# Adding the halves of attention's outputs with accumulating transfers

## The chip, the cores and the metric

The kernel runs on one core of one Trainium2 chip. A core has five engines with an instruction queue each: TensorE (PE; its weight loads are shown apart as PEld), VectorE (DVE), ScalarE (ACT), GpSimd (POOL) and SyncE (SP), and 16 DMA engines behind the queues that issue transfers (here SP, ACT and POOL). The metric is the device time of one execution in microseconds (us), lower is better.

## The reference

One layer of a hybrid decoder, 2048 tokens of width 1024 in float32: attention and pooling side by side, a gated MLP with a causal convolution, and a gated embedding. The change lies in attention. It has 8 heads of 64 channels. Each query attends to three dilated windows, and the three results are weighted by their softmax denominators:

```python
DIL_PATTERNS = ((128, 1), (512, 4), (2048, 16))
...
def _dilated_attention(q, k, v, slopes):
    """Mixture of dilations: branch outputs weighted by their softmax denominators."""
    for window, dil in DIL_PATTERNS:
        o, m, d = _dilated_branch(q, k, v, slopes, window, dil)
    ...
    w = d * jnp.exp(m - jnp.max(m, axis=0, keepdims=True))
    w = w / jnp.sum(w, axis=0, keepdims=True)
    return jnp.sum(w[..., None] * o, axis=0)
...
def reference(...):
    hn = _rmsnorm(h, ln_mix[i])
    z = hn @ w_in[i]                      # q, k, v, u
    att = _dilated_attention(q, k, v, slopes)
    pool = _multiscale_pool(u, pool_w[i], pool_scale[i])
    h = h + jnp.concatenate([att, pool], axis=-1) @ w_out[i]
    ...                                   # MLP, embedding, final norm
```

The kernel folds the second and third window into one "far" part, so that each query has a "near" and a "far" result.

## The kernel before

Three phases run one after the other: projection (to about 400 us of the span), attention (to about 698 us), and the rest. [...]

Attention walks through 128 steps: 8 heads of 16 query blocks of 128 tokens. Two heads make a pair (32 steps), and four steps make a group. `CFG["ord"]` is a table of stages with a lag each; in step `s` the loop issues, in the order of the table, every stage for the block `s - lag`. Since the schedule of this phase is manual, that is the order of each engine's queue. The stages, with the names in the profile:

- `B`, `A`: take buffers (`tt` for scores, `ee` for exponentials).
- `N`, `F`: near scores (tile `sn`, L574 and L575) and far scores (`sf`, L563 and L564) on TensorE. All near scores share one PSUM bank, in two halves.
- `nm`, `fm`: add the bias and take the minimum (the scores are negated), on VectorE (L579, L585).
- `ne`, `fe`: exponentials with their sums, on ScalarE (L591, L595), each followed by a short read of the sum.
- `T`: the exponentials are turned by TensorE in blocks of 128x128 into `tp` (L605).
- `h`, `l`: high part on ScalarE (`pth`, L618) and low part on VectorE (`ptl`, L622).
- `V`, `W`: the products with the values into `o`, 128 x 512 per group (L633 near, L647 far). A group takes four steps: parts 0 and 1 are far, parts 2 and 3 near.
- `o`, `p`: take the result out of PSUM. The values carry high and low parts side by side, so that 64 of the 128 rows of `o` have the product with one and 64 that with the other, and the two halves must be added. `o` copies the foreign 64 rows into `ev` on ScalarE (L664), and `p`, one step later, adds the head's own 64 rows on VectorE (L665) into `s1` (near) or `s3` (far). Even heads own the lower 64 rows of the pair's `s1` and `s3`, odd heads the upper 64.
- `S`: at the end of a pair the maxima and denominators are turned by TensorE and copied by VectorE (`mix_stats`, `sx` and `sy`).
- `M`: mixing of the pair before, spread over the steps of the pair that runs. With `d` the steps since that pair ended: the statistics are stored on ScalarE's queue at `d = 2` and loaded in another layout at `d = 4` (`std`, `stf`, `sn`, `sf`); VectorE makes the weights at 9 and 10; and GpSimd stores them (`wd`, L885), loads them spread over rows (`wb`, L896), multiplies `s1` and `s3` with them and adds (L906, L907, L913), splits the result (L918, L919) and stores it (L929, L930), in four chunks. In GpSimd's queue nothing stands between these but themselves.

The last pair is not mixed so: `last_near` copies its statistics on VectorE into two tiles `nr` (L811), the second of which takes the buffer `m3` of GpSimd's products; `last_far` and `last_weights` follow, and VectorE mixes it at the start of the rest.

q, k, v and the biases are loaded on SyncE's queue, one load per step, head by head (`load_qk`) and, for the values, at the steps of `V_STEPS`. A tile's next use waits until its readers are done.

Of the kernel before, what the change touches and what calls it, by code (L numbers as in the profile page):

```python
# [10 lines left out]
F32 = mybir.dt.float32  # L11
F32R = mybir.dt.float32r
AF = mybir.ActivationFunctionType
ALU = mybir.AluOpType
# [3 lines left out]
P = 128  # L18
D = 1024
KD = D // P  # L20
S = 2048
H = 8
DH = 64
# [3 lines left out]
CH = 512  # L27
# [13 lines left out]
V_N = V_CB + 2 * NF  # L41


CFG = {"tt": 2, "ee": 2, 'ord': [['B', 0], ['A', 1], ['M', 0], ['V', 7], ['fm', 1], ['W', 7], ['N', 0], ['p', 8], ['T', 2], ['F', 0], ['o', 7], ['ne', 1], ['fe', 1], ['h', 2], ['l', 3], ['S', 2], ['nm', 0]], 'perm': [3, 1, 2, 0], 'fp': [[0], [1], [2], [3]], 'np': [[0, -1], [1], [2], [3]], 'm': [9, 10, 13, 4, 6, 7]}


class Shared:
# [7 lines left out]
def rdma(nc, dst, src):  # L55
    nc.sync.dma_start(fp(dst) if dst.dtype == F32R else dst, fp(src) if src.dtype == F32R else src)
# [429 lines left out]
def phase_attention(tc, g, mx, near_b, far_b):  # L486
# [2 lines left out]

    nc = tc.nc  # L490
    NS = H * NQ
    with ExitStack() as ctx:
        sb = ctx.enter_context(tc.tile_pool(name="b_sb", bufs=1, reuse_waits="tile"))
        ps_n = ctx.enter_context(tc.tile_pool(name="b_n", bufs=1, space=PSUM, reuse_waits="tile"))
# [29 lines left out]

        def load_v(pr, which, q):

            v = sb.tile([P, 4, 2, P], F32R, tag=which, bufs=4 + (which == "v1"), name=f"{which}_{pr}_{q}")
            vals[pr, which, q] = v
            src = near_v[:, 4 * q : 4 * q + 4, pr, :] if which == "v1" else far_v[q, :, :, pr, :]
            return v.rearrange("p b h d -> p b (h d)"), src  # L530


        V_STEPS = {n: (("v3", "v1")[x], q) for x in range(2) for q, n in enumerate(((25, 29, 33, 37), (20, 31, 35, 39))[x])}

        def begin(s):
            h, n = divmod(s, NQ)
# [13 lines left out]
            st.nm1, st.nm3 = st.pt.st1[:, 0, st.e, n : n + 1], st.pt.st3[:, st.r, 0, st.e, st.i : st.i + 1]  # L550
            st.d1, st.d3 = st.pt.st1[:, 1, st.e, n : n + 1], st.pt.st3[:, st.r, 1, st.e, st.i : st.i + 1]
            st.tt = sb.tile([P, 768], F32, tag="tt", bufs=CFG["tt"], name="tt")

        def exp_tile(s):
            steps[s].ee = sb.tile([P, 768], F32, tag="ee", bufs=CFG["ee"], name="ee")

        def far_scores(s):
            st = steps[s]
# [65 lines left out]
        def near_pv(gi, kbs, first):  # L624
            gr, q0 = groups[gi], 4 * (gi % 4)
            for kb in kbs:
                if q0 + kb < 0:
                    continue
                m0, m1 = max(0, kb), min(3, kb + 1)
                b0, b1 = 4 * m0 + kb + 1, 4 * m1 + kb + 1  # L630
                kt = q0 + kb
                for pt in (gr.h, gr.l):
                    nc.tensor.matmul(  # L633
                        gr.o[:, m0 * P : (m1 + 1) * P],
                        vals[gi // 8, "v1", kt // 4][:, kt % 4, gi // 4 % 2, :],
                        pt[:, b0 : b1 + 1 : 4, :],
                        start=first,
                        stop=False,
                        skip_group_check=True,
                    )  # L640
                    first = False

        def far_pv(gi, kbs, first):
            gr = groups[gi]
            for kb in kbs:
                for pt in (gr.h, gr.l):
                    nc.tensor.matmul(  # L647
                        gr.o[:, kb * P :],
                        vals[gi // 8, "v3", gi % 4][:, kb, gi // 4 % 2, :],
                        pt[:, 6 * kb + 2 : 18 + kb : 5, :],  # L650
                        start=first,
                        stop=False,
                        skip_group_check=True,
                    )
                    first = False

        due = []

        def halves_sum(dst, o, e):

            mine = slice(DH * e, DH * e + DH)
            other = slice(DH * (1 - e), DH * (1 - e) + DH)
            ev = sb.tile([P, CH], F32, tag="ev", bufs=2, name="ev")
            nc.scalar.copy(ev[mine], o[other])  # L664
            due.append(lambda: nc.vector.tensor_tensor(dst, o[mine], ev[mine], op=ALU.add))  # L665

        def values(v):
            gi, part = v // 4, v % 4
            gr = groups[gi]
            if part % 2 == 0:  # L670
                gr.o = ps_o.tile([P, CH], F32, tag="o", name="o")
            if part < 2:
                far_pv(gi, CFG["fp"][2 * part], part == 0)
            else:
                near_pv(gi, CFG["np"][2 * part - 4], part == 2)

        def values_b(v):
            gi, part = v // 4, v % 4
            if part < 2:
                far_pv(gi, CFG["fp"][2 * part + 1], False)  # L680
            else:
                near_pv(gi, CFG["np"][2 * part - 3], False)

        def fold(v):
            gi, part = v // 4, v % 4
            if part % 2 == 0:
                return
            gr = groups[gi]
            h, q = divmod(gi, 4)
            pt, e = pairs[h // 2], h % 2  # L690
            mine = slice(DH * e, DH * e + DH)
            if part == 1:
                halves_sum(pt.s3[mine, q, :], gr.o, e)
            else:
                halves_sum(pt.s1[mine, q * CH : (q + 1) * CH], gr.o, e)
                groups.pop(gi)

        def folded(v):
            while due:
                due.pop(0)()  # L700

        def stats(s):
            if (s + 1) % (2 * NQ) == 0:
# [6 lines left out]
        def mix(s):  # L710
            for pr in range(NPAIR - 1):
                d = s - (pr + 1) * 2 * NQ
                if d == 2:
                    mix_stats_store(nc, g, pr, pairs[pr])
                if d == 4:
                    mix_stats_load(nc, g, mx, pr, pairs[pr])
                if d == CFG["m"][0]:
                    mix_lift(nc, g, mx, pairs[pr])
                if d == CFG["m"][1]:
                    mix_weights(nc, g, mx, pr, pairs[pr])  # L720
                for c in range(NCH):
# [11 lines left out]
        with tc.manual_schedule(engines=set(EN.values())):  # L733
            for dst, src in load_qk(0):
                rdma(nc, dst, src)
            for q in range(4):
                for which in ("v3", "v1"):
                    rdma(nc, *load_v(0, which, q))
            queue = []
            stages = {  # L740
                "F": far_scores, "N": near_scores, "fm": far_max, "nm": near_max, "fe": far_exp, "ne": near_exp,
                "T": turn, "h": high, "l": low, "V": values, "W": values_b, "S": stats, "M": mix, "o": fold, "p": folded, "B": begin, "A": exp_tile
            }
            for s in range(NS + 10):
                if s < NS:
                    h, n = divmod(s, NQ)
                    if n == 1 and h + 1 < H:
                        queue += load_qk(h + 1)
                    if queue:
                        rdma(nc, *queue.pop(0))  # L750
                    for pr in range(1, NPAIR):
                        if s - 2 * NQ * (pr - 1) in V_STEPS:
                            rdma(nc, *load_v(pr, *V_STEPS[s - 2 * NQ * (pr - 1)]))
                if s == NS + 2:
                    last_far(nc, g, mx, ps_t, pairs[NPAIR - 1])
                    pieces = pairs[NPAIR - 1].pieces = last_weights(nc, mx, pairs[NPAIR - 1])
                for nm, lag in CFG["ord"]:
                    if 0 <= s - lag < NS or nm == "M":
# [21 lines left out]
def mix_stats_store(nc, g, pr, pt):  # L780
    nc.scalar.dma_start(g.std[pr], pt.sx)
    nc.scalar.dma_start(g.stf[pr], pt.sy)
# [1193 lines left out]
```

## Time and profile before

| | |
|---|---|
| median of 3 runs | 2417.68 us (2416.0 to 2421.61) |
| the profiled execution | 2422.34 us, its span 2420.6 us |
| busy share of the span | PE 96%, PEld 81%, DVE 71%, ACT 47%, POOL 23% |
| granted TensorE clock | 0.99 |
| attention's scores | 399.4 to 678.6 us of the span |

The profile is of one execution, in microseconds from the start of the span. A row of a group has the line, the engine, the operation, out<-in with shapes, the count, the busy time, the mean in nanoseconds, and the idle time of the engine ahead of it with what ended it. A busy PE is pipelined, with modelled ends. SPq, ACTq and POOLq are the issues of transfers on those queues.

### The profile page before, as it was taken

What the parts mean: (1) busy time and instruction counts of PE and PEld (TensorE: products, weight loads), DVE (VectorE), ACT (ScalarE), POOL (GpSimd) and SP (SyncE); (2) the same over time, 40 slices, a digit from 0 to 9 for tenths busy, and PEclk for the clock granted to TensorE, in tenths of its full rate; (3) what the DMA queues carried; (4) which work ended last, traced back from release to release, by engine and by line L of the source; (5) the groups of instructions that cost most, each with busy time, mean ns of one, the idle gap of its engine ahead of it and who ended that gap; (6) DMA issues with size and microseconds to landing.
All of it is one profiled execution on the core that took longest, in us unless ns stands there. A gap on an engine that the chain in (4) does not pass through costs nothing.

```text
span 2420.6 us, 32492 instructions
## 1 busy us (share of the span) xinstructions
PE 2329.2 (96%) x11251; PEld 1963.2 (81%) x11251; DVE 1711.4 (71%) x2705; ACT 1140.5 (47%) x2055; POOL 547.7 (23%) x552
## 2 busy tenths in 40 slices
PE   8999999898879999999999999999999999999998
PEld 7888887888858878888888787788878888888888
DVE  6644445888872458999999998877766565755665
ACT  5433325888841135444446544444444444543332
POOL 3322221054520123334431566100020000001000
PEclk9999999999999999999999999999999999999999
DMA  7534437556556675455666787444488676654332
GB/s 233 179 138 174 163 137 268 215 198 191 186 196 232 215 251 169 167 200 191 212 203 228 267 274 263 163 151 142 136 308 271 226 253 208 218 168 158 122 100 92
DMA packets 248132, 476.05 MB, mean 197 GB/s; under 512 B 47361, under 2 KB 73793, under 8 KB 244897
## 3 DMA queue, kind: packets, MB, share of 16 engines
q1 hardware_dynamic: 198992, 385.20, 47.6%
q0 software_dynamic: 29328, 61.02, 7.3%
q10 hardware_dynamic: 19648, 27.77, 3.3%
q8 instruction: 88, 1.44, 0.3%
q14 instruction: 76, 0.61, 0.1%
HBM read 313.08 MB, written 160.73 MB: 196 GB/s over the span
## 4 chain that ended last, share of the span: by engine, by line
PE 75%; DVE 10%; DMA 4%; issue 4%; ACT 2%; POOL 0%; SPq 0%; ACTq 0%; DVEq 0%; POOLq 0%
PE ua L1324 17%; PE uc L1324 8%; PE dn L90 5%; PE dn L91 5%; PE dn L89 5%; PE ub L1324 4%; PE z L91 4%; PE z L89 4%; PE z L90 4%; PE gp L89 2%; PE gp L91 2%; PE gp L90 2%; PE o L89 2%; PE o L91 2%; PE o L90 2%
## 5 line engine op out<-in xcount | busy, mean ns | idle before, releaser
L90 PE MATMUL dn<-al,wu 128*128 128x512 f32 x616 | 240.2, 390 | 3.9 <-DVE al L85 3.8
L89 PE MATMUL dn<-ah,wu 128*128 128x512 f32 x616 | 240.0, 390 | 0.0
L91 PE MATMUL dn<-ah,wu 128*128 128x512 f32 x616 | 239.8, 389 | 0.0
L85 DVE TENSOR_TENSOR al<-ra,ah 128x512 fp32r<-128x512 f32 x154 | 105.9, 690 | 108.2 <-ACT ah L84 106.2
L89 PE MATMUL z<-hnh,wh 128*128 128x512 f32 (+1 forms) x480 | 170.3, 355 | 9.9 <-ACT hnh L252 6.2
L90 PE MATMUL z<-hnl,wh 128*128 128x512 f32 (+1 forms) x480 | 170.0, 354 | 3.1 <-DVE hnl L253 3.0
L91 PE MATMUL z<-hnh,wl 128*128 128x512 f32 (+1 forms) x480 | 169.8, 354 | 2.3 <-POOL wl L85 1.7
L84 ACT CAST ah<-ra 128x512 fp32r<-128x512 f32 x154 | 95.4, 622 | 140.7 <-PE dn L91 128.1
L90 PEld LDWEIGHTS dn<-al,wu 128*128 128x128 f32 x616 | 115.6, 188 | 29.7 <-DVE al L85 5.6
L89 PEld LDWEIGHTS dn<-ah,wu 128*128 128x128 f32 x616 | 115.6, 188 | 24.1
L91 PEld LDWEIGHTS dn<-ah,wu 128*128 128x128 f32 x616 | 115.6, 188 | 23.9
L85 DVE TENSOR_TENSOR wu<-ru,wu 128x1024 fp32r<-128x1024 f32 x88 | 133.0, 1511 | 2.4 <-ACT wu L84 2.4
L1324 PE MATMUL ua<-s4h,wu 128*128 128x512 f32 x352 | 117.0, 394 | 2.0 <-ACT uv L1572 2.0
L1324 PE MATMUL ub<-a12h,wu 128*128 128x512 f32 x352 | 116.8, 392 | 1.6 <-ACT a12h L1380 1.6
L1324 PE MATMUL ua<-s1h,wu 128*128 128x512 f32 x352 | 115.7, 390 | 2.0 <-ACT ug L1551 2.0
L1324 PE MATMUL ua<-s2h,wu 128*128 128x512 f32 x352 | 116.0, 391 | 1.0 <-ACT ug L1525 0.7
L1324 PE MATMUL uc<-a22h,wu 128*128 128x512 f32 x352 | 115.8, 390 | 0.6 <-DVE uv L1347 0.6
L85 DVE TENSOR_TENSOR wu<-rw,wu 128x512 fp32r<-128x512 f32 x149 | 101.0, 688 | 21.2 <-ACT wu L84 21.1
L1324 PE MATMUL uc<-s3h,wu 128*128 128x512 f32 x352 | 115.6, 389 | 0.0
L1324 PE MATMUL ua<-a11h,wu 128*128 128x512 f32 x352 | 115.5, 389 | 0.0
L155 DVE TENSOR_TENSOR acc<-acc,sq 128x512 f32<-128x512 f32 (+1 forms) x125 | 81.2, 649 | 43.9 <-ACT sq L154 30.2
L89 PEld LDWEIGHTS z<-hnh,wh 128*128 128x128 f32 x480 | 94.2, 196 | 22.0 <-ACT hnh L252 6.2
(336 smaller groups left out, 6644.4 us busy)
## 6 DMA issues: line engine op xcount, KB each, us to landing
ru<-in_w_up_dram SPq DMA_DIRECT2D x66, 512.0 KB, 4.2
wr<-in_w_in_dram SPq DMA_DIRECT2D x64, 256.0 KB, 4.3
rw<-in_w_down_dram SPq DMA_DIRECT2D x61, 256.0 KB, 3.7
nt<-h SPq DMA_DIRECT2D x56, 256.0 KB, 4.2
td<-t SPq DMA_DIRECT2D x22, 512.0 KB, 2.6
t<-td SPq DMA_DIRECT2D x22, 512.0 KB, 3.6
nt<-in_w_down_dram POOLq DMA_DIRECT2D x44, 256.0 KB, 5.4
ra<-oq0s SPq DMA_DIRECT2D x44, 256.0 KB, 4.1
```

The lines of the kernel that those rows point to most:

```text
L84: nc.scalar.copy(hi, src)
L85: (low or nc.gpsimd).tensor_tensor(lo, src, fp(hi), op=ALU.subtract)
L89: nc.tensor.matmul(ps, wh, ah, start=first, stop=False, skip_group_check=again)
L90: nc.tensor.matmul(ps, wh, al, start=False, stop=False, skip_group_check=again)
L91: nc.tensor.matmul(ps, wl, ah, start=False, stop=last, skip_group_check=again)
L155: nc.vector.tensor_tensor(acc[:, :n], acc[:, :n], sq[:, :n], op=ALU.add)
L1324: nc.tensor.matmul(pst, x[:, ksl], y, start=first and k == 0 and n == 0, stop=k == HK - 1 and n == 2, skip_group_check=True)
```

## The change

For all groups but the last two, the result is copied out of PSUM whole, in one instruction of 128 rows: far results on ScalarE (stage `o`), near results on VectorE (stage `p`). For an even head the copy goes straight into `s3` or `s1`, with the foreign half in the upper rows. For an odd head it goes into `ev`, and a transfer on SyncE's queue brings the own half into place. Then an accumulating transfer of GpSimd's queue (a new stage `G`, at the start of the next step) adds the foreign 64 rows to the own ones. The last two groups keep the copy and the add (`add_out`).

The table `ord` is another one: transposes stand last in the step at lag 1 instead of between near and far scores at lag 2, values have lag 6 instead of 7, `ee` is taken with `tt`, statistics are turned at lag 1 instead of 2, and stored at `d = 1`. The near values have four buffers instead of five, `ev` four instead of two, and `V_STEPS` is moved.

```diff
-CFG = {... 'ord': [['B', 0], ['A', 1], ['M', 0], ['V', 7], ['fm', 1], ['W', 7], ['N', 0], ['p', 8], ['T', 2], ['F', 0], ['o', 7], ['ne', 1], ['fe', 1], ['h', 2], ['l', 3], ['S', 2], ['nm', 0]], ...}
+CFG = {... 'ord': [['B', 0], ['G', 0], ['M', 0], ['h', 2], ['N', 0], ['F', 0], ['nm', 0], ['p', 7], ['o', 8], ['ne', 0], ['V', 6], ['fm', 0], ['l', 2], ['W', 6], ['S', 1], ['fe', 0], ['T', 1]], ...}
...
+    LAST = 4 * H - 2
...
-            v = sb.tile([P, 4, 2, P], F32R, tag=which, bufs=4 + (which == "v1"), name=f"{which}_{pr}_{q}")
+            v = sb.tile([P, 4, 2, P], F32R, tag=which, bufs=4, name=f"{which}_{pr}_{q}")
...
-        V_STEPS = {... ((25, 29, 33, 37), (20, 31, 35, 39))[x])}
+        V_STEPS = {... ((24, 28, 32, 36), (30, 34, 38, 42))[x])}
...
-        def halves_sum(dst, o, e):
-
+        shift = []
+
+        def halves(pt, gi, near):
+            h, q = divmod(gi, 4)
+            e = h % 2
             mine = slice(DH * e, DH * e + DH)
             other = slice(DH * (1 - e), DH * (1 - e) + DH)
-            ev = sb.tile([P, CH], F32, tag="ev", bufs=2, name="ev")
+            return e, mine, other, pt.s1[:, q * CH : (q + 1) * CH] if near else pt.s3[:, q, :]
+
+        def copy_out(copy, gi, near):
+
+            e, mine, other, dst = halves(pairs[gi // 8], gi, near)
+            o = groups[gi].o[near]
+            t = sb.tile([P, CH], F32, tag="ev", bufs=4, name="ev") if e else dst
+            copy(t, o)
+            if e:
+                nc.sync.dma_start(dst[mine], t[mine])
+            shift.append(lambda: nc.gpsimd.dma_start(dst[mine], t[other], accum_op=ALU.add))
+
+        def add_out(gi, near):
+            e, mine, other, dst = halves(pairs[gi // 8], gi, near)
+            o = groups[gi].o[near]
+            ev = sb.tile([P, CH], F32, tag="ev", bufs=4, name="ev")
             nc.scalar.copy(ev[mine], o[other])
-            due.append(lambda: nc.vector.tensor_tensor(dst, o[mine], ev[mine], op=ALU.add))
+            nc.vector.tensor_tensor(dst[mine], o[mine], ev[mine], op=ALU.add)
+
+        def shifts(s):
+            while shift:
+                shift.pop(0)()
...
         def fold(v):
             gi, part = v // 4, v % 4
-            ...
+            if part == 1 and gi < LAST:
+                copy_out(nc.scalar.copy, gi, False)
+
+        def folded(v):
+            gi, part = v // 4, v % 4
+            if part % 2 and gi >= LAST:
+                add_out(gi, part == 3)
+            elif part == 3:
+                copy_out(nc.vector.tensor_copy, gi, True)
...
-                if d == 2:
+                if d == 1:
                     mix_stats_store(nc, g, pr, pairs[pr])
```

Lines behind the new functions move by up to 15: L811 becomes L826, L906 becomes L921.

TensorE's queue in a step with far values. Before, the transposes (`tp`) stand between near scores (`sn`) and far scores (`sf`):

```order
L574 MATMUL sn<-ks_4374,qhh_4372 128x256
L575 MATMUL sn<-ks_4374,qll_4373 128x256
L605 MATMUL tp<-ident,ee 128x128 x6
L563 MATMUL sf<-ks_4374,qhh_4372 128x384
L564 MATMUL sf<-ks_4374,qll_4373 128x384
L647 MATMUL o<-pth,v_1_0_4587 128x512
L647 MATMUL o<-ptl,v_1_0_4587 128x512
```

The same step now:

```order
L573 MATMUL sn<-ks_4384,qhh_4382 128x256
L574 MATMUL sn<-ks_4384,qll_4383 128x256
L562 MATMUL sf<-ks_4384,qhh_4382 128x384
L563 MATMUL sf<-ks_4384,qll_4383 128x384
L646 MATMUL o<-pth,v_1_0_4567 128x512
L646 MATMUL o<-ptl,v_1_0_4567 128x512
L646 MATMUL o<-pth,v_1_0_4567 128x384
L646 MATMUL o<-ptl,v_1_0_4567 128x384
L604 MATMUL tp<-ident,ee 128x128 x4
```

Far scores follow near scores, and the transposes have moved behind the values.

VectorE's queue in an odd head, before, over one step and a half (`tt,st<-sn` is the near minimum, `tt,st<-sf` the far one, `128x1` rows read their result):

```order
L585 ISA tt,st_4771<-sf,fb_4376 128x384
L585 ISA st_4771 128x1
L665 TENSOR_TENSOR s_3995<-o,ev 64x512
L622 TENSOR_TENSOR ptl<-tp,pth 128x768
L579 ISA tt,st_4770<-sn,nb_4375 128x256
```

The same place now:

```order
L578 ISA tt,st_4781<-sn,nb_4385 128x256
L578 ISA st_4781 128x1
L670 COPY ev<-o 128x512
L584 ISA tt,st_4782<-sf,fb_4386 128x384
L584 ISA st_4782 128x1
L621 TENSOR_TENSOR ptl<-tp,pth 128x768
```

The add has gone; once in four steps a copy stands between the near and the far minimum.

GpSimd's queue at the mixing of the third pair, during the fourth. Before, from the store of the weights to the first chunk's result:

```order
L885 DMA wd_121<-wts 128x4x16
L896 DMA wb_7035<-wd_121 128x1x512
L896 DMA wb_7037<-wd_121 128x1x512
L896 DMA wb_7141<-wd_121 128x1x512
L896 DMA wb_7143<-wd_121 128x1x512
L906 TENSOR_TENSOR m_7198<-s_5707,wb_7035 128x512
L907 TENSOR_TENSOR m_7199<-s_5708,wb_7037 128x512
L913 TENSOR_TENSOR m_7198<-m_7198,m_7199 128x512
```

Now:

```order
L900 DMA wd_121<-wts 128x4x16
L673 DMA s_6659<-s_6659 64x512
L911 DMA wb_7047<-wd_121 128x1x512
L911 DMA wb_7049<-wd_121 128x1x512
L673 DMA s_6660<-s_6660 64x512
L673 DMA s_6659<-s_6659 64x512
L911 DMA wb_7151<-wd_121 128x1x512
L911 DMA wb_7153<-wd_121 128x1x512
L673 DMA s_6660<-s_6660 64x512
L673 DMA s_6659<-s_6659 64x512
L921 TENSOR_TENSOR m_7208<-s_5718,wb_7047 128x512
```

Five accumulating transfers (L673) of the pair that runs now stand between the weights and the first product, and two more stand ahead of each further chunk's products.

More of the change, by code (lines that the diff above doesn't have):

```diff
@@ L41 @@
 V_N = V_CB + 2 * NF
-CFG = {"tt": 2, "ee": 2, 'ord': [['B', 0], ['A', 1], ['M', 0], ['V', 7], ['fm', 1], ['W', 7], ['N', 0], ['p', 8], ['T', 2], ['F', 0], ['o', 7], ['ne', 1], ['fe', 1], ['h', 2], ['l', 3], ['S', 2], ['nm', 0]], 'perm': [3, 1, 2, 0], 'fp': [[0], [1], [2], [3]], 'np': [[0, -1], [1], [2], [3]], 'm': [9, 10, 13, 4, 6, 7]}
+CFG = {"tt": 2, "ee": 2, 'ord': [['B', 0], ['G', 0], ['M', 0], ['h', 2], ['N', 0], ['F', 0], ['nm', 0], ['p', 7], ['o', 8], ['ne', 0], ['V', 6], ['fm', 0], ['l', 2], ['W', 6], ['S', 1], ['fe', 0], ['T', 1]], 'perm': [3, 1, 2, 0], 'fp': [[0], [1], [2], [3]], 'np': [[0, -1], [1], [2], [3]], 'm': [9, 10, 13, 4, 6, 7]}
 class Shared:
@@ L530, in load_v @@
             return v.rearrange("p b h d -> p b (h d)"), src
-        V_STEPS = {n: (("v3", "v1")[x], q) for x in range(2) for q, n in enumerate(((25, 29, 33, 37), (20, 31, 35, 39))[x])}
+        V_STEPS = {n: (("v3", "v1")[x], q) for x in range(2) for q, n in enumerate(((24, 28, 32, 36), (30, 34, 38, 42))[x])}
         def begin(s):
@@ L552, in begin @@
             st.tt = sb.tile([P, 768], F32, tag="tt", bufs=CFG["tt"], name="tt")
-        def exp_tile(s):
-            steps[s].ee = sb.tile([P, 768], F32, tag="ee", bufs=CFG["ee"], name="ee")
+            st.ee = sb.tile([P, 768], F32, tag="ee", bufs=CFG["ee"], name="ee")
         def far_scores(s):
@@ L633, in near_pv @@
                     nc.tensor.matmul(
-                        gr.o[:, m0 * P : (m1 + 1) * P],
+                        gr.o[1][:, m0 * P : (m1 + 1) * P],
                         vals[gi // 8, "v1", kt // 4][:, kt % 4, gi // 4 % 2, :],
@@ L647, in far_pv @@
                     nc.tensor.matmul(
-                        gr.o[:, kb * P :],
+                        gr.o[0][:, kb * P :],
                         vals[gi // 8, "v3", gi % 4][:, kb, gi // 4 % 2, :],
@@ L655, in far_pv @@
                     first = False
-        due = []
-        def halves_sum(dst, o, e):
+        shift = []
+        def halves(pt, gi, near):
+            h, q = divmod(gi, 4)
+            e = h % 2
             mine = slice(DH * e, DH * e + DH)
             other = slice(DH * (1 - e), DH * (1 - e) + DH)
-            ev = sb.tile([P, CH], F32, tag="ev", bufs=2, name="ev")
+            return e, mine, other, pt.s1[:, q * CH : (q + 1) * CH] if near else pt.s3[:, q, :]
[11 more added lines that the diff above has]
+            ev = sb.tile([P, CH], F32, tag="ev", bufs=4, name="ev")
             nc.scalar.copy(ev[mine], o[other])
-            due.append(lambda: nc.vector.tensor_tensor(dst, o[mine], ev[mine], op=ALU.add))
+            nc.vector.tensor_tensor(dst[mine], o[mine], ev[mine], op=ALU.add)
+        def shifts(s):
+            while shift:
+                shift.pop(0)()
         def values(v):
@@ L670, in values @@
             if part % 2 == 0:
-                gr.o = ps_o.tile([P, CH], F32, tag="o", name="o")
+                gr.__dict__.setdefault("o", []).append(ps_o.tile([P, CH], F32, tag="o", name="o"))
             if part < 2:
@@ L685, in fold @@
             gi, part = v // 4, v % 4
[L686 to L695, printed above, removed]
+            if part == 1 and gi < LAST:
[6 more added lines that the diff above has]
+                copy_out(nc.vector.tensor_copy, gi, True)
+            if part == 3:
                 groups.pop(gi)
-        def folded(v):
-            while due:
-                due.pop(0)()
         def stats(s):
@@ L741, in phase_attention @@
                 "F": far_scores, "N": near_scores, "fm": far_max, "nm": near_max, "fe": far_exp, "ne": near_exp,
-                "T": turn, "h": high, "l": low, "V": values, "W": values_b, "S": stats, "M": mix, "o": fold, "p": folded, "B": begin, "A": exp_tile
+                "T": turn, "h": high, "l": low, "V": values, "W": values_b, "S": stats, "M": mix, "o": fold, "p": folded, "B": begin, "G": shifts
             }
@@ L757, in phase_attention @@
                 for nm, lag in CFG["ord"]:
-                    if 0 <= s - lag < NS or nm == "M":
+                    if 0 <= s - lag < NS or nm in "MG":
                         stages[nm](s - lag)
```

## Prediction

> **What bounds the kernel now.** I read the page first, then the busy times by stretch, the groups and waits of the attention stage, then its time-line at a pair boundary and at its end. The page says what a microsecond saved in attention is worth: TensorE is busy nearly throughout, so the work behind attention moves up as a whole when attention ends earlier.
>
> ```profile
> PE 2329.2 (96%) x11251; PEld 1963.2 (81%) x11251; DVE 1711.4 (71%) x2705; ACT 1140.5 (47%) x2055; POOL 547.7 (23%) x552
> 399.00:680.00 281.00, 251.03 (x1625) 234.69 (x1624) 232.86 (x734) 246.45 (x699) 109.66 (x116) 0.99 0.61 207
> 433.00:441.10 8.10, 7.80 (x54) 7.40 (x53) 6.90 (x23) 7.67 (x23) 0.00 (x0) 1.00 0.88 359
> L563 PE MATMUL sf<-ks,qhh x128: 392/522/669, 399.4 to 678.4; 128*128 128x512 f32 x32, 128*128 128x256 f32 x32, 128*128 128x384 f32 x32, 128*128 128x128 f32 x32
> PEld sn L574 <- DVE st L579: 32.4, 59, 2.0
> DVE tt L585 <- PE sf L564: 36.4, 57, 1.2
> ```
>
> The stretches list PE, PEld, DVE, ACT and POOL busy. In attention (399 to 680 us) no engine is full: PE 89%, ACT 88%, DVE 83%. The 128 score steps take 279.0 us. They are held by mutual waits: near scores (sn) wait for VectorE's near minimum, and VectorE's far minimum waits for the far scores (sf). The third row is four steps in 8.10 us.
>
> Part of the 279.0 us belongs to pair boundaries; here the near minimum of every second step, and ScalarE beside it:
>
> ```profile
> 608.74 0.42 DVE L579 CUSTOM_DVE_ANT_0 tt<-sn,nb 128x256 f32<-128x256 f32 x1
> 614.88 0.40 DVE L579 CUSTOM_DVE_ANT_0 tt<-sn,nb 128x256 f32<-128x256 f32 x1
> 619.15 0.42 DVE L579 CUSTOM_DVE_ANT_0 tt<-sn,nb 128x256 f32<-128x256 f32 x1
> 625.35 0.42 DVE L579 CUSTOM_DVE_ANT_0 tt<-sn,nb 128x256 f32<-128x256 f32 x1
> 629.84 0.41 DVE L579 CUSTOM_DVE_ANT_0 tt<-sn,nb 128x256 f32<-128x256 f32 x1
> ...
> 613.24 0.46 ACTq L781 DMA_DIRECT2D std<-sx  x1
> 620.95 0.45 ACTq L793 DMA_DIRECT2D sf<-stf  x1
> 621.45 0.58 ACT L664 COPY ev<-o 64x512 f32<-64x512 f32 x1 [3.10 <-PE sn L575]
> ```
>
> Two steps take 6.14, 4.27, 6.20 and 4.49 us. Against 4.4, a boundary costs about 1.7 us (statistics turned and copied) and 1.8 us: ScalarE's queue stands at its load of the statistics until the store has landed, 7.71 us behind the store's issue. Three boundaries make 10.6 us; the other pace is (279.0 - 10.6)/127 = 2.11 us a step.
>
> **A. The pace.** Per group and result a 64-row copy on ScalarE and a 64-row add on VectorE go; one 128-row copy comes, on ScalarE for far and on VectorE for near results.
>
> ```profile
> L664 ACT COPY ev<-o 64x512 f32<-64x512 f32 x64 | 37.1, 582 | 26.0 <-DVE st L579 8.2 <-PE o L647 6.6 <-PE sn L575 6.5
> L665 DVE TENSOR_TENSOR s<-o,ev 64x512 f32<-64x512 f32 x64 | 43.9, 686 | 6.2 <-ACT ev L664 5.3
> L1551 ACT COPY ug<-ua 128x512 f32<-128x512 f32 x44 | 25.9, 590 | 153.3 <-PE ua L1324 153.3
> L776 DVE COPY sy<-tps x3: 667/668/669, 469.5 to 613.1; 16x512 f32<-16x512 f32 x3
> ```
>
> More rows cost nothing (582 against 590 ns), so each engine does 30 copies and 4 old pairs in place of 64: ScalarE loses 37.1 - 30 x 0.590 - 4 x 0.582 = 17.1 us, VectorE 43.9 - 30 x 0.668 - 4 x 0.686 = 21.1 us. In the four steps of 8.10 us that leaves ScalarE 7.67 - 0.58 = 7.09 and VectorE 6.90 - 0.69 = 6.21, or 1.77 and 1.55 us a step. TensorE's work is unchanged: 7.80/4 = 1.95 by matmuls, whose ends are modelled, and 7.40/4 = 1.85 by weight loads.
>
> The new order keeps VectorE's and ScalarE's cycle (near minimum, far minimum, low part; exponentials, high part) but takes the transposes from between near and far scores and puts them behind the values. So far scores follow near scores at once, and the high parts no longer stand behind near scores that wait. The waits quoted above lose their cause. What is late next is TensorE itself: between 1.85 and 1.95 I take 1.90. A = 127 x (2.11 - 1.90) = -26.7 us; bounds 1.85 (-33) and 2.00, a tenth still lost to waits (-14).
>
> **B. The boundary.** Statistics are turned one step earlier and stored at step 1, still loaded at step 4: three steps of cover (5.7 us) in place of two (4.2) for the same 7.71 us. The wait shrinks by 1.5 us; I take 1 of the 1.8 us: B = -3 us; bounds 0 and -5.4.
>
> **C. GpSimd is tied to the steps.** Each accumulating transfer waits in GpSimd's queue for a copy of its step, and mixing the previous pair stands behind it. Before, mixing ran as soon as its weights were there:
>
> ```profile
> 634.74 0.77 POOL L885 DMA_DIRECT2D wd<-wts  x1 [19.26 <-DVE st L585]
> 646.09 1.31 POOL L906 TENSOR_TENSOR m<-s,wb 128x512 f32<-128x512 f32 x1
> 655.05 1.35 POOL L906 TENSOR_TENSOR m<-s,wb 128x512 f32<-128x512 f32 x1
> 664.05 1.35 POOL L906 TENSOR_TENSOR m<-s,wb 128x512 f32<-128x512 f32 x1
> 671.39 1.33 POOL L906 TENSOR_TENSOR m<-s,wb 128x512 f32<-128x512 f32 x1
> 674.33 1.28 POOL L913 TENSOR_TENSOR m<-m,m 128x512 f32<-128x512 f32 x1
> 683.71 1.27 DVE L811 COPY nr<-tpn 8x512 f32<-8x512 f32 x2 [1.13 <-PE tpn L804]
> 698.83 0.80 PE L91 MATMUL o<-mh,lwo 128*128 128x512 f32 x1 [4.36 <-DVE lwo L85]
> ```
>
> The second copy into nr (from 684.35) uses the buffer m3 that GpSimd's last addition (674.33 + 1.28 = 675.61) reads: 8.7 us of slack before. Behind that copy VectorE does the last pair's weights, and 14.5 us later the output projection runs.
>
> Now, from the store of the weights (634.74): the first product stands behind the near copy 8 steps later, 8.5 x 1.90 + 0.6 = 16.8 us in place of 11.35. From first product to last addition it was 29.52 us; six transfers now stand between. A transfer's issue is not in the trace; the nearest rows:
>
> ```profile
> L930 POOL DMA_DIRECT2D ml<-al x12 | 6.7, 562 | 0.0
> L896 POOL DMA_DIRECT2D wb<-wd x24 | 19.6, 829 | 23.0 <-issue 11.5 <-DMA wb<-wd 6.1 <-DMA wd<-wts 5.5
> mh<-ah POOLq DMA_DIRECT2D x12, 256.0 KB, 4.6
> wb<-wd POOLq DMA_DIRECT2D x24, 256.0 KB, 9.4
> v<-vn SPq DMA_DIRECT2D x16, 512.0 KB, 8.4
> L56 SPq DMA_DIRECT2D v<-vn x16: 359/366/2203, 404.7 to 620.9; - x16
> DMA to landing us min/median/max: 3.5/7.6/13.3
> ```
>
> (Groups of GpSimd's issues with their mean; issues with KB and median landing; landings of the v tiles.) A plain store takes 0.56 us of the queue, a spreading load 0.83; I take 0.7, so the last addition ends 16.8 + 29.5 + 4.2 = 50.5 us behind the weights. Left alone, the copy would come 49.6 - 22 x 0.21 - 1.9 (statistics a step earlier) = 43.1 us behind them. It is 7.4 us late, and 1.9 of that was gained: C = +5.5 us; 4.6 to 6.3 by the two rows. The issue time has no lower end in the trace (0.35 us an issue would give +3.4) and no upper one: rival 3.
>
> [...]
>
> **D. The buffers ev.** For the odd head the copy goes into ev (four buffers); a SyncE transfer moves its own half, and ev comes free when the accumulating transfer lands. In pairs 1 and 2 the third one's issue ends at 16.8 + 18.0 (two chunks, 646.09 to 664.05) + 7.3 (to 671.39) + 5 x 0.7 = 45.6 us behind the weights; landing takes 4.6 to 9.4 us (rows above, twice the bytes, though an accumulate also reads its destination). ScalarE wants the buffer at 27 x 1.90 - 1 = 50.3. The wait is 0 to 4.7 us and stops every engine through ScalarE's queue; I take the middle, D = 2 x 2.4 = +4.8 us. Pair 0 has no mixing; pair 3's wait lies inside C.
>
> [...]
>
> **What costs nothing.** SyncE issues 28 more transfers, 0.37 us of its queue each by the median of the v loads; q, k and v loads behind them wait for the same steps anyway. Near values have four buffers now, loaded 10 steps (19 us) ahead; the slowest landing was 13.3. The DMA share of 0.61 rises by about a fifth (88 transfers of 0.13 MB on 207 GB/s x 281 us = 58 MB). If that cover goes, TensorE waits for values. The order of every engine behind attention is unchanged.
>
> **Sum.** -26.7 - 3 + 5.5 + 4.8 = -19.4 us. The profiled execution (2422.34) becomes 2402.9; the median of the runs lies 4.66 lower: 2398.3.
>
> **Rivals.** 1: GpSimd keeps up. An issue takes 0.56 us and landing at most 4.6: D = 0, and with a pace of 1.85 A = -33 and C = 16.3 + 29.5 + 3.4 - 42.0 - 1.9 = 5.3. Sum -30.7, 2387. For it speaks that 64 rows are half of every quoted transfer; against it, loads of 9.4 us in the same queue.
> 2: The pace hardly changes. If TensorE, ScalarE and VectorE lock at 2.08, A = -3.8; GpSimd is then less late: C = 18.3 + 29.5 + 4.2 - 47.0 - 1.9 = 3.1, D = 0. With B the sum is -3.7, 2414. For it speaks that now 8.10 us pass where the busiest engine has 7.80.
> 3: Slower. The accumulating transfer is dear: with x us an issue and landing L, C = 1.3 + 6x and D = 2(5x + L - 8.2). With L = 8 the sum is -28.8 + 16x: from x = 1.8 us the gain is gone. At 2.5 us it is +11, 2429. Neither excluded nor shown by any row; every issue seen took under 0.86.
>
> **How the numbers follow.** My forecast (10 to 25 us faster) 0.45, rival 1 0.25, rival 2 0.14, rival 3 0.16. The predicted time is the forecast's, 2398. 2381 (A at -33, B at -5.4, C at 3.4, D at 0) to 2415 takes in rivals 1 and most of 2. Faster by over 0.2% (4.8 us, about what a measurement can tell) is the first two and a third of rival 2: 0.75; same 0.10; slower 0.15.
>
> **What would show it.** A: far minimum hardly waits for sf, steps of 1.9 us. B: ScalarE's load of statistics waits less. C: the copy into nr waits for GpSimd's addition, about 7 us. D: ScalarE's copy into ev waits for a transfer in pairs 1 and 2. I am wrong if steps stay above 2.0 us, if issues exceed 1 us or landings 10 us, or if TensorE waits for v.

## The result and the profile after

The changed kernel is slower: 2442.77 us median of 5 runs (2439.76 to 2452.46) against 2417.68 us (2416.0 to 2424.47) in the same comparison; ratio 1.0103, 95% interval [1.0077, 1.0129]. The forecast was 2398 us, faster, with 2381 to 2415 as its range. The profiled execution took 2442.42 us, its span 2440.6 us.

The page's first line, of the kernel after:

```profile
PE 2323.7 (95%) x11251; PEld 1963.5 (80%) x11251; DVE 1695.6 (69%) x2675; ACT 1117.0 (46%) x2025; POOL 599.0 (25%) x612
```

The busy times in the 281 us that were shown of before (PE, PEld, DVE, ACT, POOL; then granted clock, DMA share, GB/s), and the group of the far scores, whose first and last start bound the 128 steps:

```profile
399.00:680.00 281.00, 235.65 (x1593) 225.98 (x1592) 211.20 (x691) 219.97 (x658) 141.93 (x156) 0.93 0.85 234
```

```profile
L562 PE MATMUL sf<-ks,qhh x128: 308/431/522, 399.2 to 683.1; 128*128 128x512 f32 x32, 128*128 128x256 f32 x32, 128*128 128x384 f32 x32, 128*128 128x128 f32 x32
```

VectorE and ScalarE have less work, as said, and attention is still longer: its scores run from 399.2 to 683.1 us (283.9 in place of 279.0). The mean granted clock has fallen from 0.99 to 0.93, and the share of the DMA engines has risen from 0.61 to 0.85 for 234 in place of 207 GB/s.

Where nothing stands still, the kernel is much faster. The first of five undisturbed stretches of four steps and the sum and mean of the five, by stretch; then the two waits that carried 32.4 and 36.4 us before:

```profile
484.00:491.17 7.17, 6.95 (x49) 6.81 (x50) 6.59 (x23) 7.05 (x22) 4.30 (x6) 1.00 0.42 79
sum 36.14, PE 35.92 PEld 35.11 DVE 32.68 ACT 35.08 POOL 20.77; mean PE 7.18 PEld 7.02 DVE 6.54 ACT 7.02 POOL 4.15
```

```profile
PEld sn L573 <- DVE st L578: 8.5, 6, 2.6
DVE tt L584 <- PE sf L563: 1.1, 7, 0.2
```

36.14/20 = 1.81 us a step in place of 2.11, and the far minimum waits for far scores 1.1 us in all. The time went into a few long stops, in which all engines but GpSimd stand still. Six of the waits in attention and at its end, longest first (the engine and what it did, what it waited for, us in total, times, longest):

```profile
POOL s L673 <- DMA s<-ev: 34.8, 4, 10.0
ACT ev L670 <- DMA s<-ev: 31.9, 2, 16.5
DVE s L680 <- ACT ev L679: 15.2, 3, 11.0
POOL m L921 <- DMA wb<-wd: 12.0, 2, 6.1
ACT ev L679 <- DMA s<-ev: 9.4, 1, 9.4
DVE lo L882 <- DMA sf<-stf: 5.3, 3, 2.4
```

Twice ScalarE's copy into `ev` waits for the transfer that reads the buffer, 16.5 and 15.4 us, and once more at the end, 9.4 us. This is the first stop in the time-line of GpSimd, ScalarE and TensorE; then, by the issues with KB and median landing (the time from issue to the arrival of the data), the two transfers issued at 526.23 and the wb loads just ahead of them:

```profile
524.61 1.66 POOL L911 DMA_DIRECT2D wb<-wd  x2
526.23 1.83 POOL L673 DMA_DIRECT2D s<-ev  x2
543.74 0.59 ACT L670 COPY ev<-o 128x512 f32<-128x512 f32 x1 [16.48 <-DMA s<-ev]
544.38 0.79 PE L646 MATMUL o<-pth,v 128*128 128x512 f32 x1 [17.01 <-ACT ev L670]
```

```profile
s<-ev POOLq DMA_DIRECT2D x2, 128.0 KB, 17.4
wb<-wd POOLq DMA_DIRECT2D x2, 256.0 KB, 18.2
```

A transfer of 128 KB takes 17.4 us to land. In the busy times by stretch the stop and the restart look like this:

```profile
532.00:534.00 2.00, 0.00 (x0) 0.00 (x0) 0.00 (x0) 0.00 (x0) 1.86 (x3) 0.50 1.23 225
546.00:548.00 2.00, 2.00 (x11) 1.96 (x10) 1.35 (x4) 1.84 (x7) 1.89 (x2) 0.50 0.92 269
548.00:552.00 4.00, 4.00 (x32) 3.96 (x32) 3.31 (x13) 3.30 (x11) 3.92 (x6) 0.99 0.98 292
```

TensorE idles from 527.4. By finer stretches its granted clock is still 1.00 from 530.5 to 531.0 and 0.50 from 531.5, so it falls some 3.6 us after the last product; it comes back at 548, 3.6 us after TensorE has work again. The two steps with a stop take 19.68 and 18.57 us; less the wait and a step of 1.81 that leaves 1.4 us each for the restart.

The end of attention (GpSimd's last addition, the copy into `nr`, the first product of the output projection with the low part of its weights; `lwo`, L85, is what the copy of the weights in fp32r, L84, leaves of them):

```profile
695.26 1.26 POOL L928 TENSOR_TENSOR m<-m,m 128x512 f32<-128x512 f32 x1
699.25 1.28 DVE L826 COPY nr<-tpn 8x512 f32<-8x512 f32 x2 [1.96 <-PE tpn L819]
716.05 0.79 PE L91 MATMUL o<-mh,lwo 128*128 128x512 f32 x1 [3.99 <-DVE lwo L85]
```

From the last scores to that product it was 698.83 - 678.4 = 20.4 us; it is 716.05 - 683.1 = 33.0.

The span's +20.0 us, added up: pace 127 x (1.81 - 2.11) = -38.1; two stops 19.68 + 18.57 - 2 x 1.81 = +34.6; the rest of the boundaries 283.9 - 127 x 1.81 - 34.6 = 19.4 in place of 10.6, +8.8; the end +12.5; behind it +2.8 (2440.6 - 716.05 against 2420.6 - 698.83). That is +20.6; 0.4 of the difference is the pace of before, rounded, and 0.2 the first scores, which start at 399.2 in place of 399.4.

### The profile page after: what moved, and what is told of

It is laid out like the page before. It is cut to its first block, busy times and chain, and to the rows that moved or that the text cites. A ratio compares the mean times of both kernels' runs of the same rounds, so it can differ in the third digit from the quotient of the medians.

```text
span 2440.6 us, 32621 instructions
## 1 busy us (share of the span) xinstructions
PE 2323.7 (95%) x11251; PEld 1963.5 (80%) x11251; DVE 1695.6 (69%) x2675; ACT 1117.0 (46%) x2025; POOL 599.0 (25%) x612
## 4 chain that ended last, share of the span: by engine, by line
PE 57%; DVE 7%; DMA 3%; issue 3%; ACT 1%; POOL 0%; DVEq 0%; POOLq 0%; SPq 0%; ACTq 0%
PE ua L1339 15%; PE uc L1339 7%; PE dn L90 6%; PE dn L89 6%; PE dn L91 6%; PE ub L1339 4%; PE o L91 2%; PE o L89 2%; PE o L90 2%; PE gp L89 2%; PE gp L91 2%; PE gp L90 2%; DVE wu L85 2%; DMA oq1s<-x 1%; DMA oq1s<-yg 1%
## 5 line engine op out<-in xcount | busy, mean ns | idle before, releaser
L85 DVE TENSOR_TENSOR al<-ra,ah 128x512 fp32r<-128x512 f32 x154 | 105.8, 689 | 112.6 <-ACT ah L84 108.9
L84 ACT CAST ah<-ra 128x512 fp32r<-128x512 f32 x154 | 95.2, 621 | 147.2 <-PE dn L91 130.3
L85 DVE TENSOR_TENSOR wu<-ru,wu 128x1024 fp32r<-128x1024 f32 x88 | 133.2, 1514 | 1.8 <-ACT wu L84 1.8
L85 DVE TENSOR_TENSOR wu<-rw,wu 128x512 fp32r<-128x512 f32 x149 | 100.8, 685 | 20.2 <-ACT wu L84 20.2
```

The costliest lines, as they stand in the source:

```text
L84: nc.scalar.copy(hi, src)
L85: (low or nc.gpsimd).tensor_tensor(lo, src, fp(hi), op=ALU.subtract)
```

## The experiments

Each ratio is to before, measured in the same comparison. The diffs are against the kernel after and are shortened; "..." marks what is left out. A stop is the long step around a wait. Theory 1: the price lies in transfers that land late because of what stands ahead of them in GpSimd's queue. Theory 2: all 16 DMA engines are full, whatever the queue. A third came later.

**More buffers.**

```diff
-... tag="ev", bufs=4 ...      tag="ah", bufs=3 ...      tag="al", bufs=3 ...
+... tag="ev", bufs=7 ...      tag="ah", bufs=2 ...      tag="al", bufs=2 ...
```

> Seven buffers ev in place of four (ah and al have two in place of three to make room). Theory 1 (the two stalls of 16 to 17 us and the 9.4 us at the end are ScalarE and VectorE waiting for an ev buffer that an accumulating transfer still reads): the buffer is wanted three copies, so 6 steps or 10.9 us, later; the stalls fall to about 6 us each and the one at the end goes: 2442.8 - 2 x 10.9 - 9.4 = about 2412 us (2405 to 2418). Rival (the time is lost because GpSimd's mixing is late, and the wait for ev only passes that on): within 5 us of 2443.

2434.6 us, ratio 1.0055 [1.0034, 1.0077]: about half of the loss, and less than expected. The waits for `ev` have gone (0.4 us for a transfer are left), but there are still two stops, of 14.3 and 14.0 us, two steps later and at another wait. The longest wait in the first one, ScalarE's queue in it with the copy into `nr` much later, and the landings of all accumulating transfers (least, median, most):

```profile
ACT pth L617 <- DMA ks<-kk: 12.7, 1, 12.7
```

```profile
524.83 0.46 ACTq L796 DMA_DIRECT2D std<-sx  x1
537.99 0.37 ACTq L804 DMA_DIRECT2D sn<-std  x1
543.25 0.37 ACTq L808 DMA_DIRECT2D sf<-stf  x1
693.53 0.68 DVE L826 COPY nr<-tpn 8x512 f32<-8x512 f32 x1 [9.34 <-POOL m L928]
```

```profile
DMA to landing us min/median/max: 2.6/7.9/25.9
```

ScalarE's high part is put down to a load of k, but stands behind two loads of statistics that its own queue issues only at 537.99 and 543.25. The stores that these loads read had landed by 533.2 (525.42 and a landing of 7.8 us for the later one), so what held the loads after that stays open; the later one is issued as SyncE's 1 MB load of k lands (521.3 + 21.9 = 543.2). This wait had been hidden by the first. The transfers of GpSimd's queue land no earlier (up to 25.9 us), so buffers treat the symptom. And `nr` now does wait for GpSimd's addition.

**wb loads on SyncE's queue.**

```diff
-mix_fetch(nc, g, mx, nc.gpsimd, pr, pairs[pr], c)
+mix_fetch(nc, g, mx, nc.sync, pr, pairs[pr], c)
```

> The spread loads of the weights (wb) are issued on SyncE's queue in place of GpSimd's. Theory 1 (an accumulating transfer lands late because it stands behind the wb loads in GpSimd's one queue): it lands in 3 to 8 us, no wait for ev is left, and the time is 2442.8 - 34 - 9 = about 2400 us (2393 to 2410). Rival (the 16 DMA engines are full with the q, k and v loads then, whatever the queue): it still lands after more than 11 us, the stalls stay above 10 us each, and the time stays above 2428.

2498.62 us, 1.0311 [1.0289, 1.0333]: far from theory 1's time and, being above 2428, on the rival's side; the landings are theory 1's. The landings of the accumulating transfers, SyncE's queue, and the longest wait:

```profile
DMA to landing us min/median/max: 2.6/6.3/10.5
```

```profile
515.02 20.23 SPq L911 DMA_DIRECT2D wb<-wd  x2
```

```profile
POOL s L673 <- DMA s<-ev: 110.0, 7, 28.0
```

Accumulating transfers now land within 10.5 us, as theory 1 has it, but the wb loads hold SyncE's queue for 20 us, the own halves of odd heads stand behind them, and GpSimd's transfers wait for those. The two queues wait for each other; as a test of the time it is spoilt.

**No accumulation.**

```diff
-nc.gpsimd.dma_start(dst[mine], t[other], accum_op=ALU.add)
+nc.gpsimd.dma_start(dst[mine], t[other])
```

> The transfers of GpSimd's queue only copy the foreign half over the own one; the addition is left out. Theory 1 (place in the queue): landing times, stalls and time as with the addition, 2435 to 2446. Rival (the accumulation is what makes them slow, since it reads its destination too): landing falls below 6 us, the stalls go, about 2400.

2444.82 us, 1.0089 [1.0067, 1.011]: as expected, no gain. ScalarE's two waits for `ev` are 34.8 us. GpSimd's queue (q0: packets, MB, share of 16 engines) between 405 and 449 us, when it carries eight of these transfers and nothing else, in the kernel after and then without accumulation:

```profile
q0 software_dynamic: 640, 1.05, 13.9%
```

```profile
q0 software_dynamic: 384, 1.05, 8.8%
```

Accumulation is not free, 0.139 x 44 x 16 / 8 = 12.2 us of one DMA engine's time for 128 KB in place of 7.7, but its removal leaves the stops.

**The order alone.**

```diff
 def folded(v):   # at the place of p, lag 7
+    ...
+    nc.scalar.copy(ev[mine], groups[gi].o[part == 3][other])
 def fold(v):     # at the place of o, lag 8
+    ...
+    nc.vector.tensor_tensor(dst[mine], groups[gi].o[part == 3][mine], groups[gi].ev.pop(0)[mine], op=ALU.add)
```

> The new order of stages with the old sums: for every group a 64-row copy on ScalarE and, a step later, a 64-row add on VectorE; no transfers. If the new order alone sets the pace, a step is bound by ScalarE with one 64-row copy more in four steps, (7.05 + 0.58)/4 = 1.91 us: 2417.7 - 127 x 0.20 - 3 = about 2390 us (2385 to 2400). Rival (the shorter work of ScalarE and VectorE is what made the pace of 1.81, and the order does little): steps above 2.05 us, 2408 to 2418.

2400.03 us, 0.9907 [0.9892, 0.9922]: faster than before and after, at the upper edge of what was expected. Eight steps by stretch, the group of the far scores, and the end in the time-line:

```profile
489.68:505.00 15.32, 15.15 (x105) 14.13 (x104) 14.20 (x45) 15.13 (x45) 8.17 (x9) 1.00 0.74 250
```

```profile
L562 PE MATMUL sf<-ks,qhh x128: 335/432/522, 400.3 to 656.9; 128*128 128x512 f32 x32, 128*128 128x256 f32 x32, 128*128 128x384 f32 x32, 128*128 128x128 f32 x32
```

```profile
676.98 0.79 PE L91 MATMUL o<-mh,lwo 128*128 128x512 f32 x1 [4.03 <-DVE lwo L85]
```

1.92 us a step with ScalarE busy 15.13 of 15.32 us; scores take 256.6 us, and the end 20.1 us as before. The order by itself, with the numbers of buffers and the earlier statistics that come with it, is worth 22 us.

**Transfers for even heads alone** (no `ev` held, nothing on SyncE's queue; odd heads as in the order alone).

> Transfers for even heads alone (32 accumulating ones, none on SyncE's queue); odd heads keep the 64-row copy and the add of the order alone. Theory 1 (the price of the transfers is the odd heads': the buffers ev that wait for a landing, and the own halves on SyncE's queue): no wait for ev, even heads at 1.81 us a step, odd heads at the 2.0 of the order alone, so 64 x 0.17 = 11 us under the order alone, with some 3 us lost to GpSimd's later end: about 8 us under the order alone's ratio to before (0.991), 0.987 or 2390 us. Rival (any transfer on top of the q, k, v loads fills the 16 DMA engines and delays the rest): not faster than the order alone, ratio 0.991 to 1.0.

2408.49 us, 0.995 [0.9932, 0.9967]: a miss, and on the rival's side. No wait for `ev` is left, but one step takes 9.1 us because VectorE waits for statistics, and `nr` waits for GpSimd:

```profile
DVE lo L897 <- DMA sf<-stf: 5.6, 1, 5.6
DVE nr L841 <- POOL m L943: 3.7, 1, 3.7
```

**Loads spread.**

```diff
-if queue:
+if queue and n % 2:
     rdma(nc, *queue.pop(0))
```

> The kernel after with the five q, k and bias loads of a head at every second step in place of every step (steps 1, 3, 5, 7, 9). Theory 2 (the 16 DMA engines are full when the three 1 MB loads come together at a head's start, which delays the accumulating transfers and the statistics): the stalls of 18 to 20 us in the second and third pair fall to 10 or less, 2442.8 - 20 = about 2423. Rival theory 1 (place behind the wb loads in GpSimd's queue): landing 17 us as before, stalls as before, 2436 to 2448.

2442.7 us, 1.0094 [1.0075, 1.0113]: nothing. ScalarE's waits for `ev` are 35.3 us, and the transfers behind them take up to 20.2 us. Of a head's 1 MB loads the first stays at its step and the second moves by one step, so this says little against theory 2.

**One chunk's wb loads per pair.**

```diff
+if c:
+    pt.wb[c] = pt.first_wb
+    return
```

> The kernel after with the spread weights loaded for the first chunk alone and used for all four (three chunks get the wrong weights): 18 of 24 wb loads are left out. Theory 1 (accumulating transfers stand behind wb loads in GpSimd's queue): they land in under 9 us in the second half of a pair too, the stalls of 18 to 20 us fall under 5, about 2405 us (2398 to 2414). Rival theory 2 (engines full with q, k, v loads): landing above 11 us and stalls above 10 us each, 2428 or more.

2405.83 us, 0.9937 [0.9922, 0.9953]: as theory 1 has it. No wait for `ev` is left. Landings of the accumulating transfers, the group of the far scores, and the stretch of the first stop by busy times:

```profile
DMA to landing us min/median/max: 2.6/6.3/11.9
```

```profile
L562 PE MATMUL sf<-ks,qhh x128: 308/424/522, 400.2 to 657.5; 128*128 128x512 f32 x32, 128*128 128x256 f32 x32, 128*128 128x384 f32 x32, 128*128 128x128 f32 x32
```

```profile
530.00:590.00 60.00, 55.31 (x369) 53.25 (x369) 48.86 (x161) 51.84 (x156) 37.80 (x41) 0.94 0.88 251
```

The DMA engines are as full as in the kernel after (0.88 in both here; 1.06 against 0.96 from 524 to 544 us, around the stop), and no step takes more than 6.2 us: full engines alone do not make the stop. Yet the kernel is no faster than the order alone.

**The old order with copies and transfers.** The table of before with `G` in it, `V_STEPS` a step later, statistics stored at `d = 2`.

> The order of before with whole copies and transfers. If the mutual waits of the old order set its pace, whatever ScalarE and VectorE are spared: steps of 2.05 to 2.11 us, A at most -7; a pair takes some 7 us longer than in the kernel after, so the waits for ev shrink from 17 to about 10 us in two pairs: 2418 - 5 + 20 + 5 = about 2438 (2425 to 2448). Rival (the spared work alone gives the pace): steps of 1.95 us, 2410 to 2425.

2439.96 us, 1.0075 [1.0054, 1.0096]. The time is the one expected, the pace is the rival's. Four steps by stretch, and the wait for `ev`:

```profile
563.82:571.57 7.75, 7.66 (x54) 7.39 (x53) 6.51 (x22) 7.12 (x22) 5.24 (x7) 1.00 0.51 80
```

```profile
ACT ev L672 <- DMA s<-ev: 29.2, 3, 15.3
```

1.94 us a step. So the spared work alone brings 0.17 us a step, the order alone 0.19, both 0.30; and the transfers bring the same waits at either order.

**Another place for the wb loads.**

```diff
-'m': [9, 10, 13, 4, 6, 7]
+'m': [9, 10, 15, 4, 5, 5]
```

> The kernel after with another place of the mixing in GpSimd's queue (numbers m: 15, 4, 5, 5 for 13, 4, 6, 7): a chunk's wb loads are issued ahead of the products of the chunk before, some 7.5 us of GpSimd's work ahead of the next accumulating transfers, in place of right ahead of them. Nothing is left out and no byte is moved less. Theory 1 (place behind the wb loads): transfers that landed after 17 to 20 us land after about 10, the two stalls fall from 18 and 17 us to about 10 each and the one at the end by as much: about 2422 us (2412 to 2430). Rival theory 2 (the engines are full, whatever the place): landing and stalls as before, 2436 to 2448.

2449.45 us, 1.0098 [1.0082, 1.0113]: theory 1 in this form falls, and the time is nearer to theory 2's (2436 to 2448). The transfers that the first stop waits for, in GpSimd's time-line and by their landing, and the waits:

```profile
532.87 1.76 POOL L673 DMA_DIRECT2D s<-ev  x2
```

```profile
s<-ev POOLq DMA_DIRECT2D x2, 128.0 KB, 12.3
```

```profile
ACT ev L670 <- DMA s<-ev: 42.3, 4, 17.0
```

They land after 12.3 instead of 17.4 us, but GpSimd issues them 6.6 us later, behind its products, and they land at 545 us; in the kernel after it was 544. Hence theory 3: the queue holds a backlog, and a transfer lands when the bytes issued ahead of it have drained, wherever among them it stands. It is read from these two landings and not tested by itself. How little of that queue can move is seen in four microseconds of the kernel after, 524 to 528, by queue (q1 is SyncE's):

```profile
q1 hardware_dynamic: 522, 1.12, 100.8%
q0 software_dynamic: 26, 0.03, 4.6%
```

While two of SyncE's 1 MB loads run, GpSimd's queue gets 4.6% of the engines. That is one slice of the stop. From 536 to 540 and from 540 to 544 SyncE's queue has only 22.2% and 2.3%, and GpSimd's, with 77.9% and 51.2%, moves 0.59 and 0.47 MB; the transfers land at the end of this. The kernel with one chunk's wb loads has a slice of 4.1% as well (536 to 540), in a step of 6.2 us. So the starved slice alone does not make the long stop.

**Stores on SyncE's queue, and no q and k loads.** The first moves the mh and ml stores to the other queue, the second leaves the loads of heads 2 to 7 out.

```diff
-mix_store(nc, g, mx, nc.gpsimd, nc.gpsimd, pr, pairs[pr], c)()
+pairs[pr].__dict__.setdefault("st", {})[c] = mix_store(nc, g, mx, nc.gpsimd, nc.sync, pr, pairs[pr], c)
+if d == CFG["m"][2] + CFG["m"][3] * c + CFG["m"][5] + 6:
+    pairs[pr].st.pop(c)()
```

```diff
+if h > 1:
+    heads[h] = heads[h - 2]
+    return []
```

> The kernel after with the stores of the mixed result (mh and ml, 24 of 256 KB) on SyncE's queue, six steps later, in place of GpSimd's; the same bytes move, through another queue. Theory 3 (GpSimd's queue holds a backlog, and a transfer lands when all bytes issued ahead of it have drained, wherever it stands): some 1 MB less stands ahead of the transfers that landed after 17 to 20 us; they land after 10 or less, and the two stalls and the wait at the end fall from 17, 16 and 9 us to a few: 2405 to 2420 us. Rival theory 2 (the 16 DMA engines as a whole are full): the same bytes, the same stalls, 2434 or more.

> The kernel after without the q, k and bias loads of heads 2 to 7, which use those of heads 0 and 1 (wrong scores): 20 MB less on SyncE's queue, GpSimd's queue as it is. Theory 3 with starvation (SyncE's bursts take the DMA engines, 95 to 101% for 8 us at a time, and the backlog of GpSimd's queue drains only between them): no burst at the pair boundary, landing under 10 us, stalls under 4 us, 2400 to 2412. Rival (GpSimd's queue is slow by itself, some 0.12 MB a microsecond whatever else runs): stalls of 10 us or more stay, 2425 or more.

The first: 2446.25 us, 1.0102 [1.0085, 1.0119], the rival's time, but spoilt as the wb loads were: GpSimd waits 47.1 us for own halves on SyncE's queue, and the two stops (15.4 and 15.2 us) now stand at the place of ScalarE's stores of the statistics. It decides nothing between theories 2 and 3. The second: 2413.8 us, 0.9967 [0.9956, 0.9978], between the two expectations. Its waits for `ev` and its landings:

```profile
ACT ev L673 <- DMA s<-ev: 16.2, 2, 9.0
```

```profile
DMA to landing us min/median/max: 2.6/7.4/16.6
```

Half of the 31.9 us goes with SyncE's bursts, half stays, and the two stops are 10.4 and 12.2 us: the bursts delay GpSimd's queue, and it is slow by itself as well. The bursts themselves are shorter than was expected: in the kernel after, SyncE's queue has 92.6% of the engines from 520 to 528 us, with the 100.8% in the second half, and 62.7% in the next four.

**The first pair alone** (transfers where no mixing runs), beside the order alone again.

> Whole copies and transfers for the first pair of heads alone, where no mixing and no wb load runs; the other three pairs have the 64-row copies and adds of the order alone. Theory 1 (transfers pay where nothing slow stands ahead of them in GpSimd's queue): 32 steps of 1.81 in place of 1.945 us, 4.3 us under the order alone, ratio to before 0.989. Rival (the fuller DMA engines delay the first boundary's statistics by as much): the order alone's ratio, 0.991, or above.

> The order alone once more, beside the first-pair kernel: ratio 0.991 as before, steps of 1.945 us.

0.9907 [0.9892, 0.9923] and 0.9892 [0.9878, 0.9906] (2402.49 and 2399.04 us): no gain, the rival's result. At 462.9 us, at the end of the first pair, it is 2.7 us ahead of the first trace of the order alone; its first boundary has steps of 4.2 and 3.5 us, and at the second one it is 0.9 us behind.

**Even heads with later statistics,** `nr` in a buffer of its own, and the same without transfers.

```diff
-if d == 4:      'm': [9, 10, 13, 4, 6, 7]       nr in tag "m3"
+if d == 6:      'm': [12, 13, 15, 4, 6, 7]      nr in a tag of its own
```

> Transfers for even heads alone, with what held that kernel at its boundaries put right: statistics loaded at step 6 in place of 4, weights made at 12 and 13, first wb load at 15, and the second tile nr in a buffer of its own in place of m3. Theory (the 9.1, 5.3 and 3.6 us steps at the boundaries and the 3.7 us of nr behind GpSimd's addition were what even-head transfers cost beyond their gain): 15 us less at the boundaries, tail as before: ratio 0.985 to 0.988, some 2390 us, faster than the order alone. Rival (the fuller DMA engines give the time back at the next wait): 0.990 or above.

> The order alone with the same later statistics and the same buffer for nr, for comparison: its boundaries hardly wait for statistics (no wait above 1.7 us there), so within 3 us of the order alone, ratio 0.989 to 0.991.

0.9964 [0.9953, 0.9976] and 0.995 [0.993, 0.997] (2414.44 and 2410.53 us): both misses, and both slower than the order alone. Mixing that starts three steps later frees the halves of the pair before too late. The wait for them in each:

```profile
ACT s L670 <- POOL m L937: 11.6, 2, 6.0
```

```profile
DVE s L708 <- POOL m L926: 8.3, 2, 4.4
```

## Why the prediction was wrong

**A, the pace:** right in kind, too small. -26.7 was said with -33 as its bound; it was -38.1. The bound came from reading TensorE's busy time as a floor. Four steps had 7.80 us of matmuls and 7.40 of weight loads before, and have 7.18 and 7.02 now, for the same products: part of what is shown as busy was evidently waiting. ScalarE, taken as 7.09 us, has 7.02 of 7.23 and is as close to the bound.

**B, the boundary:** wrong, +8.8 in place of -3. The steps that became shorter also shortened the cover of the next transfer: from the load of the statistics (step 4) to their use (step 9) five steps are now 9 us, and VectorE waits 5.3 us for them, a wait that before does not have; the other 3.5 us of the 8.8 are not traced to a wait. The load's landing was not followed, only the store's.

**C, GpSimd's end:** its terms held, but its wait did not come. The last addition was put 50.5 us behind the weights; it ended 696.52 - 645.20 = 51.3 us behind them. An issue takes 0.93 us (0.96 from `ev`), where 0.7 was taken. In the kernel after the copy into `nr` comes later still (699.25) and waits for TensorE. With seven buffers `nr` does wait for the addition, 9.3 us. With one chunk's wb loads the end is 683.94 - 657.5 = 26.4 us, 6.0 over before; that this is near the 5.5 predicted proves little, since only 2.6 us of it are the wait of `nr`.

**D, the buffers:** the step that failed. It was put at 4.8 us, and the two stops cost 34.6: of the 39 us between the span that was forecast and the measured one, 30 lie here. Its working, with the measured pace and issue, is 16.0 + 18.0 + 7.3 + 5 x 0.93 + L - 47.9. With L = 17.4 that is 15.5 us a pair, and 16.5 and 15.4 were measured. That it comes so close is in part luck: the first transfer was issued at 526.23, 43.8 us behind the weights (482.43), and the wait began at 527.26, 44.8 behind them, so both ends lie 1 to 3 us earlier than in the working. The term that was mis-sized is the landing L: 4.6 to 9.4 was taken from medians of other transfers, and a buffer waits for its own landing, not for the median. The prediction had named landings over 10 us as a sign of being wrong, and they came. The trace of before had the warning, in the wb load that GpSimd issued at 501.49 us there:

```profile
wb<-wd POOLq DMA_DIRECT2D x1, 256.0 KB, 17.6
```

The least landing of the kernel after, 2.6 us, is far from the one that decides; the range of all its accumulating transfers is

```profile
DMA to landing us min/median/max: 2.6/7.8/20.8
```

Why L is as long as it is in this queue is only in part shown, as the experiments say. The last pair's wait was said to lie inside C; it came before C instead (9.4 us of ScalarE, for which VectorE's add waits 11.0) and made most of the end's 12.5 us.

**Rival 3** had the right mechanism, D = 2(5x + L - 8.2), with the price at the wrong place: it put the danger into the issue time x, and gave L = 8. **What costs nothing:** the DMA share was to rise by a fifth, to 0.73; it is 0.85. A transfer of this kind takes 12.2 us of an engine's time, where the forecast's share comes to 0.12 x 281 x 16 / 88 = 6.1; but without the accumulation, at 7.7 us, the share from 399 to 690 us is still 0.82 (with it 0.85), so the rest of the rise is not explained.

**Slips in the working:** the lower bound's own terms give 2422.34 - 35.0 - 4.66 = 2382.7, not 2381. The load of statistics at 620.95 reads the later store, issued at 613.83, so it waited for a landing of 7.1 us and not 7.71. One issue in the prediction's own rows took 2.203 us, on SyncE's queue; under 0.86 holds for GpSimd's.

Shown: the two stops of the kernel after are the wait for `ev` (even heads and one chunk's wb loads take the wait away, and the longest steps left are 9.1 and 6.2 us; seven buffers take the wait away too, but a stop of 14 us at the next wait comes in its place); the accumulation itself is not their cause; with fewer wb loads in GpSimd's queue they go, with fewer loads in SyncE's they shrink to 10.4 and 12.2 us; the order alone keeps 22 us. Argued only: that the backlog drains in order. Open: how the DMA engines share their time between the two queues, and what held ScalarE's loads with seven buffers.

## What to carry to other kernels

A buffer that comes free when a transfer lands must be covered for the queue's longest landing, under the load that the faster kernel itself makes, not for the median before: here for 20.8 us, where 4.6 to 9.4 was taken. A change that does two things is to be priced, and run, apart: here the order was worth 22 us, and the transfers cost about twice that. When steps get shorter, every cover counted in steps shrinks with them, and the next wait is found there: here five steps of cover are now 9 us, and VectorE waits 5.3 us behind them.

## What was not expected of the hardware

A transfer of 64 rows of 2 KB inside the on-chip memory takes 12.2 us of one DMA engine's time (summed over the 16) if it accumulates and 7.7 if it only copies; SyncE's loads, 11.93 MB in 75.7% of 44 us of 16 engines, need 5.9 us for the same 128 KB. Beside 1 MB loads, GpSimd's queue got 4.6% of the engines for four microseconds, with 26 packets beside 522 of SyncE's queue. Whether GpSimd's queue had a packet ready at each engine then, no row shows.

In both stops TensorE's granted clock falls to 0.50, some 3.6 us after the last product in the first (527.4 to 531.0) and 3.3 us after it in the second (609.7 to 613.0). It comes back 3.6 us after the next product in the first (544.4 to 548.0) and 5.2 us after it in the second (624.8 to 630.0).
